# Two-layer diffusion backbone on one core: values in four tiles, pooling partly on VectorE, softmax division moved to the outputs, early products moved to VectorE

## The chip, the core and the metric

The kernel runs on one core of a Trainium2 chip. A core has TensorE (PE, matrix products), VectorE (DVE), ScalarE (ACT), GpSimd (POOL) and SyncE (SP), which here issues nearly all DMAs, one after the other. The metric is the device time of one execution in microseconds; the time before is the median of three runs, 1372.81 us (1372.37 to 1374.88).

## The reference

Two layers work on 1024 latent tokens (a grid of 16 rows by 64 columns) and 256 context tokens, with 1024 features. Cut to what matters here:

```
h  = rmsnorm(x) * (1 + scale) + shift               # modulation from silu(c) @ w_mod
p  = h @ w_in                                       # one projection, split over four mixers
y  = concat(gla(p), neighbourhood_attention(p), s5(p), pool(p)) * silu(gate columns of p)
x  = x + gate * rmsnorm(y @ w_out)

neighbourhood_attention: 4 heads of 64; each latent query reads an 8 x 16 window and the 256 context
  tokens; s = q k + bias, -inf outside the window; p = softmax(s); o = p v; context queries read
  context tokens alone (layer 0 only)
pool: windows 2, 4, 8, 16 (64 features each): (centred_mean(u, w) - u) @ w_pool, times a scale;
  at the ends of the sequence the mean is over the tokens that are there
```

Layer 1 gives no context output.

## The kernel before, in words

Products in float32 are made of three products of a high and a low part each (`hi*hi`, `hi*lo`, `lo*hi`). Features that pass between stages lie in DRAM (`dP` pooling input, `dQ`, `dK`, `dN` queries, keys and values, `dG` gates, `dY` mixer outputs). A layer runs gated linear attention with the modulation products beside it (phase "mods", which reads the silu of the conditioning, `csil`, held in SBUF throughout), the S5 scan, the pooling and gate projections, then phase "na" (L1234), which this change concerns most, and phase "out". The order on each engine comes from a scheduler that lists instructions by priority, and every engine works its list in order: what stands at the head and waits holds up all behind it, SP's DMAs too.

Phase "na" has 4 heads. A job is one head and one block of 128 queries, in the order 0, 1 (context, layer 0 only), 4, 5, 2, 3, 6, 7, 8, 9: 40 jobs in layer 0, 32 in layer 1. Per job: scores on PE (L1331 into `nS`), add of the bias and row minimum on DVE (L1338; L1341 for context blocks), exponential with row sum on ACT (L1343), reciprocal of the sum (L1345) and multiplication of the 128 x 640 probabilities by it on DVE (L1346). Three jobs later PE transposes the probabilities (L1376 into `nT`, three buffers), ACT casts the high part (L1382) and DVE makes the low part (L1383). Per pair of jobs PE multiplies by the values (L1398), ACT copies one half (L1400), and DVE adds the halves into `nay` (L1412). There are 20 pairs in layer 0 and 16 in layer 1.

`na_head` loads a head's keys (L1293), queries (L1299, two buffers) and values: `naV`, one tile 128x10x128 of all ten token blocks, 640 KB, with one buffer (L1302). So the next head's values can be loaded only when the last product of this head has read the tile.

Beside the jobs, one pooling piece (256 tokens, half of the features) is made every four jobs: SP loads the input (L1453, `pu`) and the 128x256 reciprocals of the window lengths (L1455, `piv`, one buffer); POOL makes window sums (L1457 to L1463), multiplies the two halves by `piv` (L1465, L1466) and subtracts the input (L1467). PE, ACT and SP finish the piece (L1476 to L1479). There are 10 pieces in layer 0 and 8 in layer 1. In layer 0, part of the gate projections (L317, L346) fills PE between the jobs.

Two jobs before the end, `out_early` (L393) starts on the first three output tiles: `out_load` (L366) loads parts of `dY` and `dG` (L376) into freed `naK` and `naQ` buffers, multiplies them on POOL (L377), and ACT and DVE make the high and low parts (L379, L380). There are six such products a layer.

Of the kernel before, what the change touches and what calls it, by code (L numbers as in the profile page):

```python
# [12 lines left out]
F32 = mybir.dt.float32  # L13
F32R = mybir.dt.float32r
# [8 lines left out]
SEQ = 1024  # L23
# [16 lines left out]
NH = '11'  # L40
NRM = 0
PS0 = 0
# [27 lines left out]
class Kernel:  # L70
# [72 lines left out]
    def load_consts(self):  # L143
# [16 lines left out]
        self.dG = [self.dram.tile([D, NTOK], F32, name=f"dG{l}") for l in range(DEPTH)]  # L160
        self.dY = [self.dram.tile([D, NTOK], F32, name=f"dY{l}") for l in range(DEPTH)]
        self.dX = self.dram.tile([NTOK, D], F32, name="dX")
        self.dU = [self.dram.tile([NTOK, 256], F32, name=f"dU{l}") for l in range(DEPTH)]
# [9 lines left out]
    def silu_c(self):  # L173

        nc, v = self.nc, self.nc.vector
        cc, th = (self.t([128, 8, 2], "cc", 2) for _ in range(2))
        nc.sync.dma_start(cc, self.a["cc"])
        nc.scalar.activation(th, cc, AF.Tanh, scale=0.5)
        v.scalar_tensor_tensor(th, th, 1.0, cc, op0=ALU.add, op1=ALU.mult)
        v.tensor_scalar(th, th, 0.5, None, op0=ALU.mult)  # L180

        self.csil = self.const.tile([128, 4, 34], F32, name="csil")
        v.memset(self.csil, 0.0)
        for i in range(2):
            v.tensor_copy(self.csil[:, :, 32 * i:32 * i + 2], th.rearrange("p (a b) n -> p a b n", b=2)[:, :, i])

    def modulation(self, l, pieces, raws, width, psum, pool, lag=1):
# [178 lines left out]
    def out_load(self, l, t, dest, k0, n, early=None):  # L366
# [8 lines left out]
        for x, d in ((y, self.dY), (g, self.dG)):  # L375
            self.q(5).dma_start(x, d[l][k0 * 128:(k0 + n) * 128, t * 128:(t + 1) * 128].rearrange("(k p) n -> p k n", p=128))  # L376
        self.eng(4).tensor_tensor(y, y, g, ALU.mult)  # L377
        hi, lo = (x[:, ks] for x in dest)
# [906 lines left out]
    def na_head(self, l, h, last):  # L1285
# [8 lines left out]
        for piece in range(2):  # L1294
# [5 lines left out]
            Q.append(qt)  # L1300
        V = self.t([128, 10, 128], "naV", 1, dtype=F32R)
        nc.sync.dma_start(V.bitcast(F32), self.dN[l][:, h * 128:(h + 1) * 128].rearrange("(t p) e -> p t e", p=128))  # L1302
        if h % 2 == 0:
# [82 lines left out]
    def na_values(self, l, job0, job1, last):  # L1386
# [5 lines left out]
        one = [(b, 0, 128 * a, 128) for a, b in rest]  # L1392
        hi = [(V[:, b, :], o, 0, s, q, n) for b, s, q, n in both + one]
        lo = [(V[:, b, 0:64], o[0:64], 1, s, q, n) for b, s, q, n in both + one]
        todo = hi[:1] + lo[:1] + hi[len(both):] + lo[1:] + hi[1:len(both)]
        for i, (w, out, part, s, q, n) in enumerate(todo):
            x = PT[:, part, s].rearrange("p a q -> p (a q)")[:, q:q + n]
            nc.tensor.matmul(out[:, q:q + n], lhsT=w, rhs=x, start=(i == 0), stop=(i == len(todo) - 1))  # L1398
# [7 lines left out]
        if NRM:  # L1406
            for i, r in enumerate((r0, job1[2])):
                nc.tensor.transpose(ps[0:64, i * 128:(i + 1) * 128], r.to_broadcast([128, 64]), self.ident)
            nc.vector.tensor_tensor(t[0:64], o[0:64], t[64:128], ALU.add)
            nc.vector.tensor_tensor(yc, view(t[0:64]), view(ps[0:64, 0:256]), ALU.mult if NRM == 1 else ALU.divide)  # L1410
        else:
            nc.vector.tensor_tensor(yc, view(o[0:64]), view(t[64:128]), ALU.add)  # L1412
# [15 lines left out]
    def pooling(self, l, last):  # L1428
# [4 lines left out]
        wb, sc = wb[:, 0:256].rearrange("p (m n) -> p m n", m=2), wb[:, 256:258]  # L1433
        nc.sync.dma_start(sc, a["pool_sc"][l])
        nc.sync.dma_start(wb, a["pool_wb"][l].rearrange("m k n -> k m n"))
        PAD = 8
# [3 lines left out]
        for (t0, t1, lo, hi) in pieces:  # L1440
            n = t1 - t0
            W = n + 2 * PAD
            for m in range(2):
# [9 lines left out]
                nc.sync.dma_start(u[:, d0:d1], self.dP[l][m * 128:(m + 1) * 128, c0:c1])  # L1453
                iv = self.t([128, PW], "piv", 1)
                nc.sync.dma_start(iv[:, :n], a["pool_inv"][:, m, t0:t1])  # L1455

# [7 lines left out]
                rr, uu = s4[:, PAD:PAD + n], u[:, PAD:PAD + n]  # L1464
                gp.tensor_tensor(s4[0:64, PAD:PAD + n], s2[0:64, PAD:PAD + n], iv[0:64, :n], ALU.mult)  # L1465
                gp.tensor_tensor(s4[64:128, PAD:PAD + n], s4[64:128, PAD:PAD + n], iv[64:128, :n], ALU.mult)  # L1466
                gp.tensor_tensor(rr, rr, uu, ALU.subtract)  # L1467
                todo.append((m, t0, n, u, rr, wb, sc))
# [63 lines left out]
    def run(self):  # L1532
# [9 lines left out]
        for l in range(DEPTH):  # L1542
# [5 lines left out]
            with self.phase("mods", True) as pool:  # L1548
                psum = self.ps2
                pm = lambda: psum.tile([128, 512], F32, tag="pm", bufs=1, name=self.nm("pm"))  # L1550
                todo = ((1, (2,)),) if last else ((0, (2,)), (1, (1, 0)))
# [45 lines left out]
def _consts():  # L1597
# [40 lines left out]
    out["id32"] = np.tile(np.eye(32, dtype=f), (4, 1))  # L1638
    inv = np.zeros((128, 2, NTOK), f)
    for wi, w in enumerate((2, 4, 8, 16)):  # L1640
        for off, n in ((0, CTX), (CTX, SEQ)):
            t = np.arange(n)
            cnt = np.clip(t - w // 2 + w, 0, n) - np.clip(t - w // 2, 0, n)
            inv[64 * (wi % 2):64 * (wi % 2) + 64, wi // 2, off:off + n] = (f(1.0) / cnt.astype(f))[None]
    out["pool_inv"] = inv
# [96 lines left out]
```

## Time and profile before

| | us | share |
|---|---|---|
| median of three runs | 1372.81 | |
| profiled execution, its own time | 1372.72 | |
| its span | 1370.9 | |
| PE busy | 1252.5 | 91% |
| DVE busy | 913.4 | 67% |
| ACT busy | 582.7 | 43% |
| POOL busy | 202.8 | 15% |

The span is the time between the first and the last instruction of the profiled execution. Shares are means over stages with different limits. DMAs moved 228.99 MB. Phase "na" lies at about 490 to 613 us in layer 0 and 1155 to 1272 us in layer 1; its heads begin (first score minimum) at 494.4, 520.4, 546.7 and 578.9 us, and at 1163.1, 1184.5, 1205.7 and 1232.0 us.

### The profile page before, as it was taken

Reading aid. Unit: us, or ns where it says so; the run is one execution under the profiler, and the core shown is the slowest. Engines: PE = TensorE matmul, PEld = TensorE weight load, DVE = VectorE, ACT = ScalarE, POOL = GpSimd, SP = SyncE. Lnnn points to the kernel's source line nnn. Section 1 sums busy time; section 2 is a strip of 40 time slices with the busy share of each in tenths; the row PEclk is TensorE's granted clock in tenths of the full one; section 3 lists DMA queues with packets and bytes.
Section 4 is the critical chain, followed back from the end, with each engine's and each line's share of the span. In section 5 each row is a group of like instructions: output and inputs, shape, how many; then the busy total and the mean of one; then the engine's idle time right before and its main releaser. Section 6 shows DMA issues by size and latency. Waiting matters only on the chain. (4 is left out here: it accounts for less than half of the span.)

```text
span 1370.9 us, 20412 instructions
## 1 busy us (share of the span) xinstructions
PE 1252.5 (91%) x7102; PEld 1009.2 (74%) x7102; DVE 913.4 (67%) x2269; ACT 582.7 (43%) x1234; POOL 202.8 (15%) x218
## 2 busy tenths in 40 slices
PE   5799999999999999888989999999999989787897
PEld 2698967676777677777778989868767766666676
DVE  2778577546388658774875689596554884877383
ACT  2653433223333347653455642453323333665321
POOL 0100000001100024442410000000212100335220
PEclk9799999999999999999999999999999999989999
DMA  9446686752533277637742475975315434864662
GB/s 330 170 124 223 195 252 177 227 161 77 166 125 117 79 195 187 179 121 234 236 117 91 134 221 187 256 200 165 88 50 184 154 127 145 213 146 131 197 209 89
DMA packets 233846, 228.99 MB, mean 167 GB/s; under 512 B 47144, under 2 KB 196136, under 8 KB 233408
## 3 DMA queue, kind: packets, MB, share of 16 engines
q1 hardware_dynamic: 232144, 225.05, 54.4%
q10 hardware_dynamic: 1584, 2.49, 0.5%
q8 instruction: 59, 0.97, 0.3%
q14 instruction: 59, 0.48, 0.1%
HBM read 157.88 MB, written 69.62 MB: 166 GB/s over the span
## 5 line engine op out<-in xcount | busy, mean ns | idle before, releaser
L317 PE MATMUL pa<-ahi,wh 128*128 128x512 f32 (+1 forms) x664 | 172.3, 386 | 3.3 <-DVE stg L346 1.5
L317 PE MATMUL pa<-ahi,wl 128*128 128x512 f32 (+1 forms) x664 | 165.9, 378 | 0.1
L317 PE MATMUL pa<-alo,wh 128*128 128x512 f32 (+1 forms) x664 | 163.8, 377 | 0.3 <-PEq L1571 0.3
L317 PEld LDWEIGHTS pa<-ahi,wh 128*128 128x128 f32 x664 | 115.4, 192 | 28.5 <-issue 6.0
L317 PEld LDWEIGHTS pa<-alo,wh 128*128 128x128 f32 x664 | 115.8, 192 | 22.5 <-issue 4.7
L317 PEld LDWEIGHTS pa<-ahi,wl 128*128 128x128 f32 x664 | 114.3, 190 | 22.7 <-issue 5.6
L302 POOL TENSOR_TENSOR wl<-w,wh 128x1024 fp32r<-128x1024 f32 (+1 forms) x19 | 46.4, 2445 | 277.7 <-PE pa L317 177.2
L333 PE MATMUL pa<-wh,ahi 128*128 128x256 f32 (+1 forms) x480 | 79.5, 300 | 4.9 <-DVE ahi L260 3.9
L387 PE MATMUL po<-wx,ahi 128*128 128x512 f32 x312 | 79.1, 393 | 2.8 <-DVE stg L473 1.6
L301 ACT CAST wh<-w 128x1024 fp32r<-128x1024 f32 (+1 forms) x51 | 53.8, 1056 | 62.5 <-PE pa L317 39.6
L333 PE MATMUL pa<-wl,ahi 128*128 128x256 f32 (+1 forms) x480 | 79.4, 299 | 0.1
L333 PE MATMUL pa<-wh,alo 128*128 128x256 f32 (+1 forms) x480 | 77.2, 296 | 0.0
L333 PEld LDWEIGHTS pa<-wh,ahi 128*128 128x128 f32 x480 | 66.8, 194 | 10.1 <-issue 3.0
L387 PEld LDWEIGHTS po<-wx,ahi 128*128 128x128 f32 x312 | 58.8, 190 | 16.3 <-ACT ahi L379 2.0
L333 PEld LDWEIGHTS pa<-wl,ahi 128*128 128x128 f32 x480 | 67.5, 194 | 3.6 <-issue 2.5
L333 PEld LDWEIGHTS pa<-wh,alo 128*128 128x128 f32 x480 | 66.2, 193 | 3.3 <-issue 3.0
L1331 PE MATMUL nS<-naK,naQ 128*128 128x256 f32 (+1 forms) x272 | 57.6, 333 | 11.4 <-DVE nast L1338 6.6
L1398 PE MATMUL nT<-naPT,naV 128*128 128x256 f32 (+3 forms) x368 | 58.1, 298 | 9.9 <-DMA naV<-dN 9.2
L1338 DVE CUSTOM_DVE_ANT_0 naP<-nS,nab 128x640 f32<-128x640 f32 (+1 forms) x64 | 50.2, 785 | 18.7 <-PE nS L1331 13.8
L1398 PEld LDWEIGHTS nT<-naPT,naV 128*128 128x128 f32 (+1 forms) x368 | 49.6, 176 | 15.4 <-issue 7.7
L1376 PE MATMUL nT<-c_ident,naP 128*128 128x128 f32 x320 | 51.5, 286 | 9.4 <-DVE nay L1412 3.9
L1383 DVE TENSOR_TENSOR naPT<-nT,naPT 128x512 fp32r<-128x512 f32 (+1 forms) x104 | 56.2, 559 | 5.7 <-ACT naPT L1382 5.3
(396 smaller groups left out, 2550.5 us busy)
## 6 DMA issues: line engine op xcount, KB each, us to landing
w<-in_w_in_dram SPq DMA_DIRECT2D x41, 512.0 KB
wm<-in_w_mod_dram SPq DMA_DIRECT2D x32, 512.0 KB
s5R<-dR SPq DMA_DIRECT2D x16, 960.0 KB
xt<-in_tok_dram SPq DMA_DIRECT2D x20, 512.0 KB
wm<-in_w_mod_dram SPq DMA_DIRECT2D x8, 1024.0 KB
dR<-sp_R SPq DMA_DIRECT2D x16, 512.0 KB
dG<-stg SPq DMA_DIRECT2D x32, 256.0 KB
w<-in_w_out_dram SPq DMA_DIRECT2D x16, 512.0 KB
```

Of the source, the lines that this page charges most:

```text
L301: nc.scalar.copy(hi, raw)
L302: (next(engines) if engines else self.eng(2)).tensor_tensor(lo, raw, hi.bitcast(F32), ALU.subtract)
L317: nc.tensor.matmul(ps[:, :t1 - t0], lhsT=w(k), rhs=x[:, k, t0:t1], start=(i == 0), stop=(i == 23))
L333: nc.tensor.matmul(ps[:, :n], lhsT=x[:, k, t * 128:(t + 1) * 128], rhs=w(k), start=(i == 0), stop=(i == 23))
L387: self.nc.tensor.matmul(o, lhsT=x[:, k], rhs=m(k), start=first and i == 0, stop=last and i == len(todo) - 1)
L1331: nc.tensor.matmul(self.na_s[:, c * 128:(c + n) * 128], lhsT=Qb[:, i, :], rhs=K[:, b * 128:(b + n) * 128], start=(i == 0), stop=(i == 1))
L1338: v.tensor_tensor_reduce(P[:, 0:nk], ps, self.na_b[:, b0:b0 + nk], 1.0, -NEG, ALU.add, ALU.min, nm)
L1376: nc.tensor.transpose(ps[:, i * 128:(i + 1) * 128], P[:, c * 128:(c + 1) * 128], self.ident)
L1383: (nc.gpsimd if RLO == "p" and len(src) < 4 else nc.vector).tensor_tensor(lo, pv, hi.bitcast(F32), ALU.subtract)
L1398: nc.tensor.matmul(out[:, q:q + n], lhsT=w, rhs=x, start=(i == 0), stop=(i == len(todo) - 1))
```

## The change

Five edits. (1) `naV` becomes four tiles: blocks 0 and 1 (`naVc`, two buffers), 2 to 4 (`naVa`), 5 and 6 (`naVb`), 7 to 9 (`naVd`), each with its own load. (2) `NRM = 1`: probabilities are not multiplied by the reciprocal; instead PE transposes the two reciprocals of a pair into the first half of an `nT` tile, ahead of the pair's value products, and DVE multiplies the sum of the two output halves (`nat`) by them. (3) Pooling: one 128x34 load of `piv` a layer instead of one load a piece; on POOL only 64x8 multiplications at the ends of the sequence stay of the last three operations, and two DVE operations of 64x256 a piece scale and subtract. (4) The products of the early output tiles go to DVE. (5) `csil` is stored to DRAM (`dC`) once and loaded again in each phase "mods". Tiles that are held no longer or are smaller free room in SBUF.

```diff
-NRM = 0
+NRM = 1
@@ silu_c
-        self.csil = self.const.tile([128, 4, 34], F32, name="csil")
+        self.csil = self.t([128, 4, 34], "csil", 1)
...
+        nc.sync.dma_start(self.dC, self.csil)
@@ out_load
-        self.eng(4).tensor_tensor(y, y, g, ALU.mult)
+        (nc.vector if early else self.eng(4)).tensor_tensor(y, y, g, ALU.mult)
@@ na_head
-        V = self.t([128, 10, 128], "naV", 1, dtype=F32R)
-        nc.sync.dma_start(V.bitcast(F32), self.dN[l][:, h * 128:(h + 1) * 128].rearrange("(t p) e -> p t e", p=128))
+        parts = ((0, 2, "naVc", 2), (2, 3, "naVa", 1), (5, 2, "naVb", 1), (7, 3, "naVd", 1))
+        V = {}
+        for b, n, tag, bufs in parts:
+            x = self.t([128, n, 128], tag, bufs, dtype=F32R)
+            nc.sync.dma_start(x.bitcast(F32), self.dN[l][b * 128:(b + n) * 128, h * 128:(h + 1) * 128].rearrange("(t p) e -> p t e", p=128))
+            V.update((b + i, x[:, i]) for i in range(n))
@@ na_values
+        if NRM:
+            for i, r in enumerate((r0, job1[2])):
+                nc.tensor.transpose(ps[0:64, i * 128:(i + 1) * 128], r.to_broadcast([128, 64]), self.ident)
...
         if NRM:
-            for i, r in enumerate((r0, job1[2])):
-                nc.tensor.transpose(ps[0:64, i * 128:(i + 1) * 128], r.to_broadcast([128, 64]), self.ident)
             nc.vector.tensor_tensor(t[0:64], o[0:64], t[64:128], ALU.add)
             nc.vector.tensor_tensor(yc, view(t[0:64]), view(ps[0:64, 0:256]), ALU.mult if NRM == 1 else ALU.divide)
@@ pooling
+        iv = self.t([128, 2, 17], "piv", 1)
+        nc.sync.dma_start(iv, a["pool_inv"])
...
-                iv = self.t([128, PW], "piv", 1)
-                nc.sync.dma_start(iv[:, :n], a["pool_inv"][:, m, t0:t1])
...
-                gp.tensor_tensor(s4[0:64, PAD:PAD + n], s2[0:64, PAD:PAD + n], iv[0:64, :n], ALU.mult)
-                gp.tensor_tensor(s4[64:128, PAD:PAD + n], s4[64:128, PAD:PAD + n], iv[64:128, :n], ALU.mult)
-                gp.tensor_tensor(rr, rr, uu, ALU.subtract)
+                for p, x in ((slice(0, 64), s2), (slice(64, 128), s4)):
+                    for c, w, there in ((PAD, 0, t0 == lo), (PAD + n - 8, 8, t1 == hi)):
+                        if there:
+                            gp.tensor_tensor(x[p, c:c + 8], x[p, c:c + 8], iv[p, m, w:w + 8], ALU.mult)
+                    nc.vector.scalar_tensor_tensor(rr[p], x[p, PAD:PAD + n], iv[p, m, 16:17], uu[p], op0=ALU.mult, op1=ALU.subtract)
@@ run, phase "mods"
+                self.csil = self.t([128, 4, 34], "csil", 1)
+                nc.sync.dma_start(self.csil, self.dC)
```

How the order changes is shown at three places; a number behind a tile's name is its instance. The first is SP in layer 1 around the last head's load of the values. Before, the load of `naV` stands behind a load of `piv`:

```order
L376 DMA naK_18567<-dG_88 128x4x128
L1453 DMA pu_18337<-dP_107 128x272
L1231 DMA nab_17612<-in_na_bias_dram 128x256
L1479 DMA dY_90<-pu_18199 128x256
L376 DMA naQ_18573<-dY_90 128x2x128
L1455 DMA piv_18468<-in_pool_inv_dram 128x256
L1302 DMA naV_18221<-dN_97 128x10x128
L1453 DMA pu_18463<-dP_107 128x264
```

After, in the same place, with the four loads spread among the others:

```order
L1308 DMA naVc_18269<-dN_98 128x2x128
L1423 DMA dY_90<-nay_17676 64x1024
L1301 DMA naQ_18266<-dQ_100 64x2x640 x2
L1308 DMA naVa_18271<-dN_98 128x3x128
L1233 DMA nab_17650<-in_na_bias_dram 128x256
L1490 DMA dY_90<-pu_18125 128x256
L378 DMA naK_18624<-dY_90 128x4x128
L378 DMA naK_18624<-dG_88 128x4x128
L1463 DMA pu_18393<-dP_108 128x272
L1308 DMA naVb_18273<-dN_98 128x2x128
...
L1490 DMA dY_90<-pu_18250 128x256
L1308 DMA naVd_18275<-dN_98 128x3x128
```

No load of `piv` stands between them, and the context part stands ahead of the head's second query load.

The second place is DVE at the end of layer 1's jobs. Before, from a multiplication of probabilities (`naP`) on; `stn` and `alo` are low parts of the early output tiles:

```order
L1346 TENSOR_SCALAR naP_18505<-naP_18505,nast_18506 128x640
L1338 ISA naP_18559,nast_18560<-nS_17618,nab_17612 128x640
L1338 ISA nast_18560 128x1
L1345 RECIPROCAL nast_18524<-nast_18524 128x1
L1412 TENSOR_TENSOR nay_17958<-nT_18496,nat_18541 64x2x16x8
L1346 TENSOR_SCALAR naP_18523<-naP_18523,nast_18524 128x640
L1383 TENSOR_TENSOR naPT_18511<-nT_18551,naPT_18511 128x128
L380 TENSOR_TENSOR stn_18566<-naQ_18573,stn_18565 128x256
L1345 RECIPROCAL nast_18560<-nast_18560 128x1
```

After, from the score minimum (L1345 there) of the last job but one on:

```order
L1345 ISA naP_18617,nast_18618<-nS_17656,nab_17650 128x640
L1345 ISA nast_18618 128x1
L379 TENSOR_TENSOR naQ_18630<-naQ_18630 128x256
L1390 TENSOR_TENSOR naPT_18660<-nT_18661,naPT_18660 128x4x128
L379 TENSOR_TENSOR naK_18636<-naK_18636 128x512
L1355 RECIPROCAL nast_18618<-nast_18618 128x1
L382 TENSOR_TENSOR stn_18623<-naQ_18630,stn_18622 128x256
L382 TENSOR_TENSOR alo<-naK_18636,ahi 128x4x128
L1345 ISA naP_18672,nast_18673<-nS_17656,nab_17650 128x512
L1345 ISA nast_18673 128x1
L379 TENSOR_TENSOR naQ_18642<-naQ_18642 128x256
L1417 TENSOR_TENSOR nat_18706<-nT_18609,nat_18706 64x256
```

The multiplications L1346 are gone, and three products with the gates (L379), each of which needs a DMA, stand among the last two score minima and the transposes' low parts.

The third place is PE in layer 1, where a pair's values begin. Before, the rest of the pair's transposes, other work, and the values:

```order
L1376 MATMUL nT_17980<-c_ident,naP_17850 128x128
L1376 MATMUL nT_17980<-c_ident,naP_17868 128x128
L1376 MATMUL nT_17996<-c_ident,naP_17904 128x128 x4
L1331 MATMUL nS_17618<-naK_17700,naQ_17706 128x384 x2
L1331 MATMUL nS_17618<-naK_17700,naQ_17706 128x256 x4
L1331 MATMUL nS_17618<-naK_17700,naQ_17706 128x384 x2
L1398 MATMUL nT_17980<-naPT_17912,naV_17709 128x256
L1398 MATMUL nT_17980<-naPT_17912,naV_17709 64x256
```

After:

```order
L1383 MATMUL nT_18158<-c_ident,naP_18042 128x128
L1383 MATMUL nT_18158<-c_ident,naP_18059 128x128
L1338 MATMUL nS_17656<-naK_17991,naQ_17994 128x384 x2
L1338 MATMUL nS_17656<-naK_17991,naQ_17994 128x256 x2
L1383 MATMUL nT_18173<-c_ident,naP_18097 128x128 x4
L1383 MATMUL nT_18207<-c_ident,naP_18114 128x128 x4
L1405 MATMUL nT_18158<-c_ident,nast_18043 64x128
L1405 MATMUL nT_18158<-c_ident,nast_18060 64x128
L1408 MATMUL nT_18158<-naPT_18102,naVb_17754 128x256
L1408 MATMUL nT_18158<-naPT_18102,naVb_17754 64x256
```

Two transposes of a reciprocal (L1405) come in ahead of the values, into the tile that the rest's transposes used.

## Rows read from the trace of the kernel before

**Rows 1.** Stretches of seven heads: start:end, length, busy PE PEld DVE ACT POOL, clock, DMA.

```profile
494.40:520.40 26.00, 24.28 (x155) 20.05 (x153) 22.36 (x54) 17.57 (x41) 11.24 (x13) 1.00 0.82 204
520.40:546.70 26.30, 24.84 (x161) 20.53 (x161) 22.62 (x58) 17.82 (x46) 9.39 (x14) 1.00 0.68 176
546.70:578.90 32.20, 27.46 (x182) 23.00 (x181) 23.75 (x63) 20.25 (x48) 14.74 (x18) 1.00 0.71 184
578.90:605.50 26.60, 25.40 (x167) 21.30 (x166) 23.29 (x60) 19.91 (x48) 10.62 (x16) 1.00 0.44 132
1184.50:1205.70 21.20, 17.25 (x118) 14.22 (x118) 18.47 (x48) 14.54 (x36) 3.58 (x5) 1.00 0.75 200
1205.70:1232.00 26.30, 21.25 (x118) 18.33 (x118) 19.80 (x48) 16.11 (x39) 8.65 (x12) 0.81 0.62 149
1232.00:1258.30 26.30, 19.66 (x118) 17.31 (x118) 19.41 (x47) 15.53 (x38) 12.69 (x17) 0.87 0.53 145
```

**Rows 2.** PE's waits, 490 to 620 us: waiting line, releaser, total us, times, longest.

```profile
PE nT L1476 <- POOL ps L1467: 3.8, 1, 3.8
PE nT L1398 <- DMA naV<-dN: 3.1, 2, 2.4
```

**Rows 3.** PE's waits, 1155 to 1276 us.

```profile
PE nT L1398 <- DMA naV<-dN: 6.1, 3, 4.4
PE nS L1331 <- DVE nast L1338: 5.6, 10, 1.3
PE nT L1476 <- POOL ps L1467: 2.8, 1, 2.8
PE nS L1331 <- DMA naQ<-dQ: 2.7, 4, 0.9
```

**Rows 4.** The DMA queue's (SP's) waits, 1155 to 1275 us.

```profile
SPq L1455 <- POOL ps L1466: 20.2, 5, 5.7
```

**Rows 5.** Chain that ended last, 1200 to 1272 us: start, us, what.

```profile
1216.45 4.68 DMA naV<-dN
...
1232.47 3.74 DMA naK<-dG
...
1242.07 0.73 POOL ps L1466
1243.21 5.24 DMA naV<-dN
```

**Rows 6.** Lines by form, 490 to 620 us: count, busy, mean ns, idle before.

```profile
L1346 DVE TENSOR_SCALAR naP<-naP,nast 128x640 f32<-128x640 f32 x24 | 18.7, 777 | 0.2
L1412 DVE TENSOR_TENSOR nay<-nT,nat 64x256 f32<-64x256 f32 x20 | 8.3, 417 | 13.1 <-ACT nat L1400 12.7
L1346 DVE TENSOR_SCALAR naP<-naP,nast 128x512 f32<-128x512 f32 x8 | 4.6, 579 | 0.1
L1346 DVE TENSOR_SCALAR naP<-naP,nast 128x256 f32<-128x256 f32 x8 | 2.8, 354 | 0.5
L346 DVE SCALAR_TENSOR_TENSOR stg<-stg,pa 128x256 f32<-128x256 f32 x3 | 1.3, 421 | 0.9 <-ACT stg L345 0.9
```

**Rows 7.** Lines by form, 1155 to 1280 us.

```profile
L1346 DVE TENSOR_SCALAR naP<-naP,nast 128x640 f32<-128x640 f32 x24 | 14.9, 622 | 0.4
L1346 DVE TENSOR_SCALAR naP<-naP,nast 128x512 f32<-128x512 f32 x8 | 5.4, 676 | 0.1
L380 DVE TENSOR_TENSOR alo<-naK,ahi 128x512 fp32r<-128x512 f32 x2 | 1.4, 681 | 0.0
L380 DVE TENSOR_TENSOR stn<-naK,stn 128x512 fp32r<-128x512 f32 x1 | 1.1, 1130 | 0.0
```

**Rows 8.** Timeline of PE around 1200 to 1206 us, two rows of transposes.

```profile
1202.90 0.82 PE L1376 MATMUL nT<-c_ident,naP 128*128 128x128 f32 x6
1204.08 0.66 PE L1376 MATMUL nT<-c_ident,naP 128*128 128x128 f32 x4 [0.35 <-DVE nay L1412]
```

**Rows 9.** Timeline of POOL around 1238 us, one row.

```profile
1238.41 0.87 POOL L1461 TENSOR_TENSOR ps<-ps 128x269 f32<-128x269 f32 x1
```

More of the change, by code (lines that the diff above doesn't have):

```diff
@@ L161, in load_consts @@
         self.dY = [self.dram.tile([D, NTOK], F32, name=f"dY{l}") for l in range(DEPTH)]
+        self.dC = self.dram.tile([128, 4, 34], F32, name="dC")
         self.dX = self.dram.tile([NTOK, D], F32, name="dX")
@@ L1392, in na_values @@
         one = [(b, 0, 128 * a, 128) for a, b in rest]
-        hi = [(V[:, b, :], o, 0, s, q, n) for b, s, q, n in both + one]
-        lo = [(V[:, b, 0:64], o[0:64], 1, s, q, n) for b, s, q, n in both + one]
+        hi = [(V[b], o, 0, s, q, n) for b, s, q, n in both + one]
+        lo = [(V[b][:, 0:64], o[0:64], 1, s, q, n) for b, s, q, n in both + one]
         todo = hi[:1] + lo[:1] + hi[len(both):] + lo[1:] + hi[1:len(both)]
+        if NRM:
+            for i, r in enumerate((r0, job1[2])):
+                nc.tensor.transpose(ps[0:64, i * 128:(i + 1) * 128], r.to_broadcast([128, 64]), self.ident)
         for i, (w, out, part, s, q, n) in enumerate(todo):
@@ L1638, in _consts @@
     out["id32"] = np.tile(np.eye(32, dtype=f), (4, 1))
-    inv = np.zeros((128, 2, NTOK), f)
+    inv = np.zeros((128, 2, 17), f)
+    t = np.r_[0:8, SEQ - 8:SEQ]
     for wi, w in enumerate((2, 4, 8, 16)):
[L1641 to L1644, printed above, removed]
+        cnt = np.clip(t - w // 2 + w, 0, SEQ) - np.clip(t - w // 2, 0, SEQ)
+        at = inv[64 * (wi % 2):64 * (wi % 2) + 64, wi // 2]
+        at[:, 0:16], at[:, 16] = w * (f(1.0) / cnt.astype(f)), 1.0 / w
     out["pool_inv"] = inv
```

## The prediction

> **What bounds the kernel now.** I read the windows by head first, then the waits of PE and of SP, the chain that ended last, and the lines kept apart by shape. In the windows (busy microseconds of PE, weight loads, DVE, ACT and POOL, then the mean granted clock, the DMA share and GB/s) the reader is to see two layers with different limits [rows 1]. In layer 0 PE is busy 24.28 to 27.46 us of heads that last 26.0 to 32.2, since gate projections fill it: 102 of 111 us. Nothing else there is as full. In layer 1, where no filler is left, PE is busy 17.25 to 21.25 us of 21.2 to 26.3, and DVE 18.47 to 19.80: a head of 21.2 us is paced by the round of scores, minimum, exponential and multiplication, and PE waits 5.6 us for the score minimum [rows 3].
>
> Three of the seven heads are longer than their neighbours. The third of layer 0 lasts 32.2 us beside 26.0, 26.3 and 26.6 (mean 26.3): 5.9 over. The last two of layer 1 last 26.3 beside 21.2: 5.1 each. Together 16.1 us [rows 1]. What ends PE's idle time in them is the load of the values: 3.1 us in layer 0 [rows 2] and 6.1 in layer 1, with a longest of 4.4 [rows 3], and the chain runs through that load twice, 4.68 and 5.24 us [rows 5]. Behind the second stands a story of three queues: POOL waits for the gates of an early output tile (3.74 us in the chain), so its pooling multiplication by `piv` ends late at 1242.8, SP stands at the next load of `piv` until then, and `naV` is right behind it, issued at 1243.21 [rows 5]. In that layer SP stands 20.2 us at such loads in five waits [rows 4]. The mean granted clock is 1.00 in five heads, 0.81 and 0.87 in the last two [rows 1]: a part of these two ran at 1.2 instead of 2.4 GHz, after PE had stood. That is inside the 16.1.
>
> **The change part by part.** The sum is made against the profiled execution, 1372.7 us (span 1370.9 and 1.8 around it), which is within 0.1 us of the median, 1372.8.
>
> *Values in four tiles, and no `piv` load a piece.* Each part of `naV` is free when its own blocks have been read, so the next head's first pair finds its blocks 0, 1 and 3 to 6 loaded while the present head still works on 7 to 9, and SP has nothing of POOL's ahead of them. The cost to be removed lies between PE's direct waits, 3.1 + 6.1 = 9.2 us [rows 2, 3], and the whole excess, 16.1. What is late next is the query tile: PE waits 2.7 us for `naQ` in layer 1 [rows 3], whose buffers don't change. So I take -11, the direct waits and a quarter of the rest. Three more DMAs a head on SP, 24 in all, stand in place of 18 loads of `piv`: nothing.
>
> *Division on the outputs and pooling on DVE.* Layer 0 loses 18.7 + 4.6 + 2.8 = 26.1 us of multiplications and gains a second output operation a pair, 20 x 0.417 = 8.3 [rows 6]. For the scale-and-subtract of 64x256 there is no row; the 128x256 one of L346 takes 0.421 [rows 6], and I use it for 20 of them: 8.4. Three products with the gates at the price of the low parts, which read two SBUF tensors too, some 0.42 to 0.68 [rows 6, 7]: 3.3 for six, half of them within these jobs, 1.7. Net -7.7. Layer 1 loses 14.9 + 5.4 = 20.3 [rows 7] and gains 16 x 0.417 + 16 x 0.421 + 3.3 = 16.7: -3.6. In layer 1 DVE is in the pacing round, so I count -3.5 (bounds -3.6 and 0). In layer 0 PE is the limit, so DVE's gain is worth 0 (bound -7.7) as long as PE has filler.
>
> *PE's two added transposes a pair.* A row of six transposes takes 0.82 us and one of four 0.66 [rows 8]: between (0.82 - 0.66)/2 = 0.08 and 0.82/6 = 0.14 each, taken 0.11. Layer 0: 40 x 0.11 = 4.4; layer 1: 32 x 0.11 = 3.5. In layer 1 they lie in PE's 4 to 7 idle us a head: 0. In layer 0 they would add to a full engine; against them, transposes of the probabilities no longer wait for L1346, and PE's 9 us of idle time there are to be filled. I set them against DVE's gain of that layer: 0, bounds -3 and +4.4.
>
> *A longer hold of `nT`.* The transposed reciprocals lie in the tile of the rest of the pair until the second output operation has read them, one operation (0.417) later. With 36 pairs that is 15.0 us if each were waited for, 0 if the other two buffers cover it. Taken +1, nearer to the cover.
>
> *Tails.* The last pooling piece ends each layer's jobs: PE waits 3.8 and 2.8 us for L1467 [rows 2, 3]. Three POOL operations of 0.73 [rows 5] with small gaps, 2.4, go; two edge multiplications of 64x8 (no row; between 0 and 0.73, taken 0.2) and two on DVE, 0.84, come: -1.2 a layer, -2.4 (bounds -6.6, all that PE waits there, and 0).
>
> *Early products on DVE.* Work of 3.3 us a layer is counted above. New is the wait: a load of gates not yet landed now stops DVE, and behind it in DVE's list are the last score minimum and low parts, for which ACT, PE and so the end wait. One stand of the full length costs 3.74, what the chain shows for such a load [rows 5]; there are 12 products. Bounds 0 and 44.9; since SP is freed of its 20.2 us of standing, the loads go out earlier, and I take +1.5 a layer, +3.
>
> *`csil` through DRAM.* No row shows it. The modulation products wait for weights anyway; 0, at most two loads of 3.74 by the row of the gates' load.
>
> Sum: -11 - 3.5 + 0 + 0 + 1 - 2.4 + 3 = -12.9, so 1372.7 - 12.9 = 1359.8 us.
>
> The low part of a `naK` tile took 1130 ns instead of 681 [rows 7] while POOL's L1461 took 0.87 us [rows 9]: both engines slow down when DVE reads two tensors from SBUF beside POOL's work. The Trainium skill says so of the two engines' shared SBUF interfaces (GPSIMD Engine Reference, 8. Key points: contention with VectorE instructions that have two SBUF inputs). The trace agrees, with these numbers. It speaks against the change, which adds only operations of that kind; rival C prices it.
>
> **The rivals.** A: *the queries take the place of the values.* `naQ` has two buffers for two pieces a head, and PE already waits for it [rows 3]. If half of the 11 us comes back there, the sum is -7.4: 1365.3. Against it: in the long heads PE's idle time names `naV` far more than `naQ`.
>
> B, the slower side: *DVE stands at the products.* With no wait at all there the sum would be -15.9; each full stand takes 3.74 away, so from five full stands of the 12 the kernel is slower. With six, one per product of one layer, it is 1372.7 - 15.9 + 22.4 = 1379.2. For it: the products of layer 1 stand in DVE's list ahead of the last score minimum, and the trace has POOL waiting for just these loads. Against: POOL came to them early because it was idle; DVE comes to them when it has worked off its list.
>
> C: *contention.* If the 36 scale-and-subtract operations and 12 products were all stretched by 1130/681 = 1.66 [rows 7], layer 1 alone would pay 16 x 0.28 + 3.3 x 0.66 = 6.7 on the pacing engine, the sum is -6.2, and the time 1366.5. Against: POOL keeps fewer operations, two to four of five to seven a piece besides those at the ends, so there is less to collide with.
>
> D: *the parts come no earlier.* If SP's list holds the four loads until the last block of the old head is read, nothing is gained but small terms: 1371, no change. Against: the order shows the first part ahead of the queries and the last one well behind it.
>
> **How the numbers follow.** Forecast 0.50, A 0.16, C 0.10, D 0.09, B 0.15. A measurement of this kernel tells a change of 0.2% (2.7 us) from none. Forecast, A and C lie beyond that: faster 0.76; D: same 0.09; B: slower 0.15. The lowest sum is the whole excess, DVE's gain in both layers and the tails: -16.1 - 3.6 - 7.7 - 2.4 = -29.8, 1343; the likeliest case's own range is 1350 to 1367 (the excess in full, or the direct waits with the transposes on top). For 8 in 10 I go from 1346 to 1374, which takes in A, C, D and B up to four stands.
>
> **What would show it.** Right: the three long heads shrink to 27 us or less in layer 0 and 22 in layer 1 at clock 1.00; no wait of PE for `naVa` to `naVd` over 1 us; SP no longer stands at `piv`; DVE's busy time falls by some 11 us; PE's waits for the last pooling piece fall below 3 us. Wrong: DVE idle before L379 for a DMA by more than 10 us in the two phases together (B); PE's wait for `naQ` above 8 us (A); mean time of the 64x256 operations above 0.6 us (C). If layer 0 gets longer by about 4 us with the long head gone, the transposes were not covered.

## The result, and the profile after

The changed kernel takes 1382.1 us (median of five runs; four lie between 1378.16 and 1383.63, one of 2001.92 us stands far off and is not in the ratio). The ratio to the kernel before is 1.0061, with an interval of 1.0039 to 1.0083: about 8 us slower, where 13 us faster was forecast and 1374 was the upper end of the range. The profiled execution took 1378.2 us, 5.4 more than that of before.

What was to go did go. PE's waits for `naV` [rows 2, 3] are not in the lists any more, and SP's standing at `piv` [rows 4] is gone; in layer 1 SP stands 9.9 us at the four loads of the values (L1308) instead, until PE has read the old blocks. But PE waits elsewhere. PE's waits of the changed kernel, 490 to 625 us (waiting line, releaser, total us, times, longest), with L1338 the scores, L1345 the score minimum, L1383 the transposes, L1405 those of the reciprocals, L1487 the pooling product and L1418 the second output operation:

```profile
PE nS L1338 <- DVE nast L1345: 4.8, 5, 1.6
PE nT L1487 <- DVE nay L1418: 3.7, 2, 2.1
PE nT L1383 <- DVE nay L1418: 3.6, 2, 1.9
PE nT L1405 <- DVE naPT L1390: 2.7, 2, 2.0
```

And 1160 to 1280 us, the first two:

```profile
PE nS L1338 <- DVE nast L1345: 13.3, 10, 3.8
PE nT L1383 <- DVE naPT L1390: 4.3, 3, 3.0
```

All of these name DVE. In layer 1 the wait for the score minimum was 5.6 us before [rows 3] and is 13.3 now, with a longest of 3.8 for 1.3; e4 will show that the longest wait tells more here than the sum. The eight heads in the changed kernel (start:end, length, busy time of PE, weight loads, DVE, ACT and POOL, then the clock, DMA share, GB/s):

```profile
492.40:519.80 27.40, 25.45 (x161) 22.10 (x160) 18.71 (x51) 16.29 (x39) 7.88 (x15) 0.94 0.69 176
519.80:549.80 30.00, 26.48 (x174) 21.90 (x173) 21.43 (x57) 20.11 (x48) 4.89 (x12) 1.00 0.68 181
549.80:581.40 31.60, 28.24 (x186) 24.31 (x185) 24.91 (x63) 18.55 (x47) 7.53 (x9) 0.95 0.56 153
581.40:610.50 29.10, 25.74 (x169) 21.23 (x167) 20.75 (x55) 18.86 (x45) 4.39 (x9) 1.00 0.37 104
1169.90:1192.60 22.70, 16.45 (x92) 13.62 (x93) 15.06 (x41) 12.51 (x29) 4.68 (x10) 0.78 0.67 179
1192.60:1214.10 21.50, 17.61 (x128) 15.39 (x129) 17.80 (x47) 15.97 (x39) 1.25 (x2) 1.00 0.69 185
1214.10:1240.00 25.90, 19.47 (x127) 17.51 (x127) 18.89 (x50) 15.38 (x36) 3.87 (x6) 0.87 0.56 140
1240.00:1262.90 22.90, 18.89 (x127) 16.98 (x126) 19.39 (x49) 15.26 (x36) 4.50 (x10) 0.93 0.49 138
```

Against [rows 1]: the third head of layer 0 is hardly shorter (31.6 for 32.2), the other three are longer (27.4, 30.0, 29.1 for 26.0, 26.3, 26.6), although DVE is busy less in them. In layer 1 only the last head gains much (22.9 for 26.3). POOL is busy for 1.25 to 7.88 us a head, so it does not lack time. The mean granted clock is below 1.00 in five of the eight heads; before it was in two of the seven shown.

The stall is seen in a stretch of the third head, at the piece that holds DVE longest of the 18. Timeline of the changed kernel, 553 to 559 us (start, us, engine, line, operation, and in brackets idle time and its releaser); the scores that the minimum at 558.52 reads were issued at 553.36:

```profile
553.36 0.87 PE L1338 MATMUL nS<-naK,naQ 128*128 128x384 f32 x4
554.04 0.64 POOL L1465 TENSOR_TENSOR ps<-pu 128x271 f32<-128x271 f32 x1 [10.82 <-DMA pu<-dP]
554.64 2.37 POOL L304 TENSOR_TENSOR wl<-w,wh 128x1024 fp32r<-128x1024 f32 x1
555.02 2.27 DVE L1478 SCALAR_TENSOR_TENSOR ps<-ps,piv,pu 64x256 f32<-64x256 f32 x1
557.09 0.68 POOL L1467 TENSOR_TENSOR ps<-ps 64x256 f32<-64x256 f32 x1
557.80 0.48 DVE L1478 SCALAR_TENSOR_TENSOR ps<-ps,piv,pu 64x256 f32<-64x256 f32 x1 [0.51 <-POOL ps L1467]
558.52 0.81 DVE L1345 CUSTOM_DVE_ANT_0 naP<-nS,nab 128x640 f32<-128x640 f32 x1
559.38 0.83 ACT L1350 ACTIVATE naP<-naP,nast 128x640 f32<-128x640 f32 x1 [2.64 <-DVE nast L1345]
```

DVE comes to a piece's two scale-and-subtracts (L1478) while POOL is at the weights' low part (L304), 2.37 us long, which stands ahead of the pooling sum L1467. The first one, which takes 0.48 us alone, takes 2.27 and ends 0.28 us after L304; the second waits for L1467. The score minimum behind them starts some 4 us after its scores have ended. POOL itself was late because the piece's input was: it stood 10.82 us for the load of `pu`, which SP issued at 551.02.

PE can pay for a stand twice: it waits, and then it runs slower. In layer 1 two scale-and-subtracts start at 1223.43, after 1.09 us of idle time for POOL's L1470. The score minimum follows at 1225.02, and PE, which stood 3.82 us for it (the longest of its waits above), goes on at 1225.91. From then on its granted clock is 0.50 (1.2 instead of 2.4 GHz) for 4 us (columns as above):

```profile
1222.00:1226.00 4.00, 0.18 (x2) 0.09 (x1) 2.82 (x6) 0.88 (x3) 1.99 (x3) 0.79 0.66 200
1226.00:1230.00 4.00, 4.00 (x18) 3.93 (x19) 3.17 (x8) 2.62 (x6) 1.25 (x2) 0.50 0.56 146
```

For all 36 scale-and-subtracts (lines by form, 488 to 625 us and, in the second fence, 1165 to 1280 us: count, busy, mean ns, idle before):

```profile
L1478 DVE SCALAR_TENSOR_TENSOR ps<-ps,piv,pu 64x256 f32<-64x256 f32 x20 | 12.7, 637 | 9.8 <-POOL ps L1477 7.7 <-POOL ps L1470 1.2 <-POOL ps L1467 0.5
```

```profile
L1478 DVE SCALAR_TENSOR_TENSOR ps<-ps,piv,pu 64x256 f32<-64x256 f32 x16 | 9.3, 581 | 4.8 <-POOL ps L1470 2.5 <-POOL ps L1477 1.6 <-POOL ps L1465 0.4
```

They hold DVE for 12.7 + 9.8 + 9.3 + 4.8 = 36.6 us, where the prediction had 15.1 (36 x 0.421) and no wait.

### The profile page after: what moved, and what is told of

Read it like the earlier page. It is cut to its first block, busy times and chain, and to the rows that moved or that the text cites. A ratio compares the mean times of both kernels' runs of the same rounds, so it can differ in the third digit from the quotient of the medians.

```text
span 1376.4 us, 20582 instructions
## 1 busy us (share of the span) xinstructions
PE 1253.6 (91%) x7174; PEld 1016.0 (74%) x7174; DVE 919.0 (67%) x2281; ACT 583.5 (42%) x1234; POOL 151.6 (11%) x176
## 5 line engine op out<-in xcount | busy, mean ns | idle before, releaser
L319 PE MATMUL pa<-alo,wh 128*128 128x512 f32 (+1 forms) x664 | 160.9, 375 | 0.3 <-PEq L1584 0.3
L319 PEld LDWEIGHTS pa<-alo,wh 128*128 128x128 f32 x664 | 116.0, 191 | 22.9 <-issue 4.5
L1338 PE MATMUL nS<-naK,naQ 128*128 128x256 f32 (+1 forms) x272 | 60.3, 344 | 21.5 <-DVE nast L1345 18.1
L304 POOL TENSOR_TENSOR wl<-w,wh 128x1024 fp32r<-128x1024 f32 (+1 forms) x19 | 46.6, 2457 | 271.9 <-PE pa L319 154.0
L335 PE MATMUL pa<-wl,ahi 128*128 128x256 f32 (+1 forms) x480 | 76.4, 294 | 0.1
L1338 PEld LDWEIGHTS nS<-naK,naQ 128*128 128x128 f32 x272 | 43.1, 204 | 34.4 <-DVE nast L1345 27.6
L1383 PE MATMUL nT<-c_ident,naP 128*128 128x128 f32 x320 | 52.8, 289 | 11.5 <-DVE nay L1418 5.0
L1350 ACT ACTIVATE naP<-naP,nast 128x640 f32<-128x640 f32 (+1 forms) x64 | 51.5, 805 | 26.5 <-DVE nast L1345 23.9
L1389 ACT CAST naPT<-nT 128x512 fp32r<-128x512 f32 (+1 forms) x104 | 48.0, 488 | 28.6 <-PE nT L1383 25.3
```

Of the source, the lines that this page charges most:

```text
L304: (next(engines) if engines else self.eng(2)).tensor_tensor(lo, raw, hi.bitcast(F32), ALU.subtract)
L319: nc.tensor.matmul(ps[:, :t1 - t0], lhsT=w(k), rhs=x[:, k, t0:t1], start=(i == 0), stop=(i == 23))
L335: nc.tensor.matmul(ps[:, :n], lhsT=x[:, k, t * 128:(t + 1) * 128], rhs=w(k), start=(i == 0), stop=(i == 23))
L1338: nc.tensor.matmul(self.na_s[:, c * 128:(c + n) * 128], lhsT=Qb[:, i, :], rhs=K[:, b * 128:(b + n) * 128], start=(i == 0), stop=(i == 1))
L1350: nc.scalar.activation(P[:, 0:nk], src, AF.Exp, bias=nm, scale=-1.0, accum_out=l1)
L1383: nc.tensor.transpose(ps[:, i * 128:(i + 1) * 128], P[:, c * 128:(c + 1) * 128], self.ident)
```

## The experiments

Twelve kernels ran. A ratio is to runs of the kernel before made beside them, with its 95% interval; 1% is 13.7 us, and a difference of two ratios is uncertain by 4 to 6 us. Theory 1: DVE stands for POOL at the scale-and-subtract. Theory 2: the division on the outputs costs PE and `nT`. Theory 3: the wait for the values only moved.

| run | what it is | ratio | interval |
|---|---|---|---|
| e1 | values in four tiles, small `piv`, `csil` reloaded; pooling on POOL | 0.9924 | 0.9901 to 0.9946 |
| e2 | division on the outputs, `csil` reloaded | 1.0076 | 1.0051 to 1.0101 |
| e3 | new pooling alone | 1.0000 | 0.9984 to 1.0017 |
| e4 | all, pooling arithmetic back on POOL | 0.9891 | 0.9870 to 0.9912 |
| e5 | `csil` reloaded alone | 1.0019 | 0.9997 to 1.0040 |
| e6 | e4, early products on POOL | 0.9935 | 0.9911 to 0.9959 |
| e7 | all, scale-and-subtract written a step later | 0.9961 | 0.9942 to 0.9980 |
| e8 | e4, `csil` rebuilt | 0.9866 | 0.9833 to 0.9898 |
| e9 | e8 without the division | 0.9881 | 0.9850 to 0.9911 |
| e10 | small `piv` alone, pooling on POOL | 0.9946 | 0.9926 to 0.9966 |
| e11 | division alone, `csil` rebuilt | 1.0065 | 1.0038 to 1.0092 |
| e12 | all but the division | 1.0007 | 0.9981 to 1.0033 |

**e1.** The values in four tiles, with the small `piv` and the reloaded `csil` of the change; the division is left out, the products stay on POOL, and the pooling arithmetic is POOL's as before:

```diff
-                    nc.vector.scalar_tensor_tensor(rr[p], x[p, PAD:PAD + n], iv[p, m, 16:17], uu[p], op0=ALU.mult, op1=ALU.subtract)
+                    gp.tensor_tensor(s4[p, PAD:PAD + n], x[p, PAD:PAD + n], iv[p, m, 16:17].to_broadcast([64, n]), ALU.mult)
+                gp.tensor_tensor(rr, rr, uu, ALU.subtract)
```

> The kernel before with the values in four tiles, csil through DRAM, and one small piv load a layer, but with all pooling arithmetic left on POOL (L1465 to L1467 stay, the factor read as one column). Theory 1 (DVE stands for POOL at the scale-and-subtract, and that ate the values' gain): this has the values' gain and no new DVE work, so 1362 to 1366 us. Theory 2 (the division on the outputs costs PE and nT buffers): also 1362 to 1366. Theory 3 (the values' wait only becomes another wait, the queries' or the scores'): 1370 to 1374, as before.

Measured 0.9924, -10.4 us. Theory 3 falls: the gain that was forecast for the values and `piv`, 11 us, is there.

**e2.** The kernel before with `NRM = 1` and the transposes ahead of the values, as in the change.

> The kernel before with the division moved to the outputs alone (and csil through DRAM, for room). Theory 1: DVE loses more than it gains and nothing waits for POOL, 1368 to 1373 us. Theory 2: the 72 added transposes, which stand ahead of the values and wait for the low part, and the longer hold of nT cost 4 to 9 us, 1377 to 1382. Theory 3: 1371 to 1375.

Measured 1.0076, +10.4 us. The division by itself costs, as theory 2 has it, or else the reload of `csil` does, which was in this kernel too; e11 parts them.

**e3.** The kernel before with the change's pooling.

> The kernel before with the new pooling alone (one piv load a layer, 36 scale-and-subtracts of 64x256 on DVE). Theory 1: DVE stands 10 us or more ahead of these for POOL, score minima come later, 1375 to 1381 us. Theories 2 and 3: the SP queue's standing at piv is gone and POOL does less, 1366 to 1372.

Measured 1.0000, neither range, although DVE does stand 11.6 us in front of the 36 operations, as theory 1 expects. e10 shows why.

**e4.** The changed kernel with the diff of e1.

> The changed kernel with the scale-and-subtract put back on POOL (three operations a piece as before, the factor read as one column of the small piv), all other edits kept. Theory 1: the DVE waits for POOL go, 1363 to 1370 us, faster than both kernels. Theory 2: no more than 2 us from the changed kernel, 1378 to 1382. Theory 3: 1374 to 1378, the difference to before being the early products and the transposes.

Measured 0.9891, -15.0 us, and 23 us faster than the changed kernel (1.0061 - 0.9891 = 0.0170). Two operations a piece on DVE, made three on POOL again, turn the result round. PE's waits of e4, 488 to 625 us, all of them:

```profile
PE nS L1338 <- ACT naP L1350: 1.5, 3, 1.0
PE nT L1488 <- POOL ps L1479: 1.2, 1, 1.2
PE nT L1383 <- DVE nay L1418: 1.1, 2, 0.9
PE nT L1488 <- DVE naPT L1390: 0.2, 1, 0.2
```

Nothing is left of the 4.8 us for the minimum, and the holds of `nT` until L1418 are 1.1 us for 7.3. The heads of layer 0 in e4:

```profile
497.10:519.30 22.20, 22.10 (x153) 19.06 (x151) 16.44 (x47) 16.18 (x40) 6.30 (x10) 1.00 0.77 197
519.30:545.40 26.10, 25.05 (x170) 21.11 (x169) 19.49 (x54) 19.58 (x48) 14.16 (x29) 1.00 0.84 215
545.40:570.70 25.30, 24.52 (x163) 20.41 (x162) 19.66 (x54) 18.63 (x45) 12.19 (x18) 1.00 0.60 162
570.70:595.90 25.20, 24.76 (x175) 21.69 (x174) 17.99 (x50) 17.47 (x44) 9.64 (x17) 1.00 0.51 148
```

PE is busy for 96.4 of 98.8 us, at a clock of 1.00. The third head, 32.2 us before, is 25.3. (Part of the gate projections runs outside these heads in e4, 660 instructions of PE for 690, so not all of the 19.3 us between the two kernels' heads is waiting.)

In layer 1 the jobs, from the first score minimum to the last output operation, last 110.2 us in the changed kernel and 97.1 in e4:

```profile
1169.90:1280.10 110.20, 86.27 (x532) 74.33 (x533) 81.40 (x204) 65.68 (x153) 17.71 (x34) 0.88 0.54 146
1162.20:1259.30 97.10, 78.41 (x529) 67.28 (x530) 71.93 (x188) 65.98 (x153) 34.66 (x58) 0.95 0.61 165
```

PE is busy 7.9 us longer in the changed kernel for nearly the same number of instructions, at a mean clock of 0.88 for 0.95. That is more than half of the 13.1 us between the two. The sum of the waits for the score minimum is not what went. In e4, 1155 to 1285 us, it is:

```profile
PE nS L1338 <- DVE nast L1345: 11.7, 15, 1.6
```

The longest fell from 3.8 to 1.6, the sum only from 13.3 to 11.7. All seven kernels with the division have 10.6 to 13.3 us of this wait in layer 1, and all seven without it 5.0 to 7.6. So its rise from 5.6 us comes with the division and is no measure of the loss.

**e5.** The kernel before with `csil` through DRAM.

> The kernel before with csil stored to DRAM and loaded again in each phase mods, nothing else. In the runs so far all kernels with this edit need 111 to 113 us from the first to the last part of layer 1's linear attention (first L933 to last L959), those without it 106. If the reload is the cause: 105.9 to 112 us in that stretch and 1376 to 1381 us in all. If it is chance or comes from another edit: 106 us and 1371 to 1376.

Measured 1.0019, with an interval that holds 1: by the time alone, inconclusive. By the trace it is in layer 1's linear attention: its first part and its last one in the kernel before, in e5 and in e8 (timeline; a transpose at the head, one at the end, idle time in brackets):

```profile
921.44 0.27 PE L933 MATMUL pb<-c_ident,KB 128*128 128x128 f32 x1
...
1027.15 0.44 PE L959 MATMUL pb<-c_ident,sq 128*128 128x128 f32 x2 [0.19 <-DVE s5st L699]
```

```profile
917.71 0.27 PE L935 MATMUL pb<-c_ident,KB 128*128 128x128 f32 x1
...
1029.27 0.44 PE L961 MATMUL pb<-c_ident,sq 128*128 128x128 f32 x2 [1.98 <-DVE sq L958]
```

```profile
914.06 0.33 PE L939 MATMUL pb<-c_ident,KB 128*128 128x128 f32 x1 [0.18 <-DVE KB L1010]
...
1020.75 0.44 PE L965 MATMUL pb<-c_ident,sq 128*128 128x128 f32 x2 [0.21 <-DVE s5st L705]
```

105.7 us before, 111.6 with the reload, 106.7 with `csil` rebuilt. PE waits 2.0 us for DVE at the end of it in e5, 0.2 in the other two. The stretch is 111 to 113 us in e1, e2, e4, e6, e7, e12 and the changed kernel too, which all reload, and 106 to 107 in the ones that don't. With the load the scheduler lists the modulation's products, the projections and the linear attention's parts in another order. That the order is the cause is argued from the two lists, not shown.

**e6.** e4 with the products on POOL:

```diff
-        (nc.vector if early else self.eng(4)).tensor_tensor(y, y, g, ALU.mult)
+        self.eng(4).tensor_tensor(y, y, g, ALU.mult)
```

> The kernel of e4 (all edits, pooling arithmetic on POOL) with the early output tiles' products on POOL as before. If DVE stands at the products' loads (the rival of the prediction): faster than e4 by 3 us or more, 1350 to 1356. If the products on DVE keep POOL free for the pooling: slower than e4, 1361 to 1366. If neither: 1358 to 1360.

Measured 0.9935: 6 us slower than e4 (0.9935 - 0.9891), a little beyond the uncertainty. The products on DVE are a gain. POOL in e6, timeline 596 to 626 us:

```profile
602.88 0.72 POOL L1479 TENSOR_TENSOR ps<-ps,pu 128x256 f32<-128x256 f32 x1
622.29 0.74 POOL L379 TENSOR_TENSOR naQ<-naQ 128x256 f32<-128x256 f32 x1 [18.69 <-DMA naQ<-dG]
```

POOL stands 18.69 us for one load there. But the last pooling piece of the layer was done by then (L1479 at 602.88), so this stand held up no pooling. How the products on DVE gain is not shown. In the changed kernel DVE is idle only 3.6 us in front of all twelve products (line L379, the share of the gates' loads):

```profile
  DMA naQ<-dG: 2.0, 2
  DMA naK<-dG: 1.6, 1
```

**e7.** The two scale-and-subtracts of a piece are written at the start of the next pooling step:

```diff
-                    nc.vector.scalar_tensor_tensor(rr[p], x[p, PAD:PAD + n], iv[p, m, 16:17], uu[p], op0=ALU.mult, op1=ALU.subtract)
+                    due.append((rr[p], x[p, PAD:PAD + n], iv[p, m, 16:17], uu[p]))
...
+                for x in due:
+                    nc.vector.scalar_tensor_tensor(*x, op0=ALU.mult, op1=ALU.subtract)
+                due = []
```

> The changed kernel with each piece's two scale-and-subtracts written one pooling step (four jobs) later, so that they come later in DVE's list; the same work. Theory 1 in the form that DVE's standing for POOL (14 us of idle time in front of them in the changed kernel) delays the score minima: less idle there and 1366 to 1374 us. In the form that the work itself and the two engines' sharing of SBUF costs the time: idle time falls but the time stays at 1378 to 1384. Theory 2 (the division): no change, 1378 to 1384.

Measured 0.9961, 13.7 us faster than the changed kernel with the same work on the same engines. So some 14 of the 23 us hang on the place in the lists. Lines by form in e7, 488 to 625 us, the main form and the one of the last piece, then 1155 to 1290 us:

```profile
L1455 DVE SCALAR_TENSOR_TENSOR ps<-ps,piv,pu 64x256 f32<-64x256 f32 x18 | 9.6, 533 | 4.1 <-POOL pu L1463 1.9 <-POOL ps L1473 1.7 <-POOL ps L1481 0.3
L1486 DVE SCALAR_TENSOR_TENSOR ps<-ps,piv,pu 64x256 f32<-64x256 f32 x2 | 1.0, 500 | 3.8 <-POOL ps L1481 3.8
```

```profile
L1455 DVE SCALAR_TENSOR_TENSOR ps<-ps,piv,pu 64x256 f32<-64x256 f32 x14 | 7.5, 532 | 1.3 <-POOL ps L1468 1.1
L1486 DVE SCALAR_TENSOR_TENSOR ps<-ps,piv,pu 64x256 f32<-64x256 f32 x2 | 1.0, 500 | 1.0 <-POOL ps L1481 1.0
```

In all the idle time falls from 14.6 to 10.2 us; 4.8 of the 10.2 stand at the last piece (L1486), which comes after the last score minimum. Between the jobs 5.4 us are left (L1455). The mean falls from 637 and 581 ns to 533 and 532. Other instructions move in the lists too when these do, so the 13.7 us are not all shown to be this idle time's. What the other 9.6 us of the 23 are, the added work, its stretching beside POOL or the standing that is left, no run parts.

**e8.** `csil` built again in each phase "mods" from a 128x8x2 tile:

```diff
-                self.csil = self.t([128, 4, 34], "csil", 1)
-                nc.sync.dma_start(self.csil, self.dC)
+                self.csil_make()   # memset and two copies on DVE, from the compact tile
```

> The kernel of e4 with the silu kept in a compact tile (128x8x2) and csil built again from it by three small DVE operations in each phase mods, no DRAM. If the reload of csil costs 4 to 6 us in layer 1's linear attention: 1353 to 1356 us. If the cost is one of the scheduler's order that any new instruction there brings: 1358 to 1360, with the stretch still at 111 us.

Measured 0.9866, median 1354.2 us, the lowest ratio of all and faster than both kernels. Its interval overlaps that of e4, so the 3 us between them are likely by the trace of the stretch, not proved by the time.

**e9.** e8 with `NRM = 0`.

> The kernel of e8 (values in four tiles, early products on DVE, pooling arithmetic on POOL with a small piv, csil rebuilt) with the probabilities multiplied on DVE (L1346) as before. If the division on the outputs gains by shortening DVE's part of a job (net 5.7 us in layer 0, 8.4 in layer 1 by the rows): 1358 to 1364, slower than e8. If the added transposes and the longer hold of nT cost more than that: 1346 to 1352, faster than e8. If neither: 1353 to 1356.

Measured 0.9881: no difference from e8 that the intervals show. Beside the other edits of e8 the division on the outputs is worth nothing that can be told either way, although it takes 14.5 us of work off DVE in layer 0's jobs and 12.0 in layer 1's (94.23 and 85.75 us busy in e9, 79.71 and 73.73 in e8).

**e10.** The kernel before with the small `piv` and the diff of e1.

> The kernel before with one small piv load a layer and all pooling arithmetic still on POOL. Measures what SP's standing at piv is worth without new DVE work. If e3 came out even because two effects cancelled (SP freed, DVE standing): 1362 to 1369. If SP's standing cost nothing: 1371 to 1375.

Measured 0.9946, -7.4 us. e3 differs from it only in the engine of the scale-and-subtract: that costs 7.4 us (1.0000 - 0.9946), and e3 was even because two effects cancelled. In e10 PE's wait for `naV` in layer 1 has fallen from 6.1 us [rows 3] to 0.2, with the values still in one tile; the first and the last line of its waits, 1155 to 1276 us:

```profile
PE nS L1333 <- DVE nast L1340: 5.8, 9, 1.3
...
PE nT L1403 <- DMA naV<-dN: 0.2, 1, 0.2
```

**e11.** e2 with e8's `csil`.

> The kernel before with the division on the outputs, csil rebuilt on DVE instead of reloaded, nothing else: e2 without the reload. If e2's 1.0076 was the division's: 1378 to 1384. If it was mostly the reload's: 1371 to 1376. By the prediction's own sum it would be 1369 to 1373.

Measured 1.0065, +8.9 us: the division's own. PE's waits of e11, 488 to 625 us, the first line, and 1155 to 1290 us, the first and the fourth:

```profile
PE nT L1409 <- DMA naV<-dN: 8.6, 2, 6.3
```

```profile
PE nS L1339 <- DVE nast L1346: 13.0, 15, 2.1
...
PE nT L1409 <- DMA naV<-dN: 2.2, 2, 1.4
```

In layer 0 the wait for the values is 8.6 us where it was 3.1 [rows 2], since SP stands at `piv` as before (19.4 us there). In layer 1 it is 2.2 where it was 6.1 [rows 3], and the wait for the score minimum has risen instead. Beside the other edits of e8 the division costs nothing (e8 against e9), so theory 2 holds only in some surroundings. Which wait makes the 8.9 us here is open.

**e12.** The changed kernel with `NRM = 0`.

> The changed kernel with the probabilities multiplied on DVE as before (no division on the outputs), all else as changed: scale-and-subtract on DVE, values in four tiles, early products on DVE, csil reloaded. If DVE's standing for POOL is the loss by itself: 1377 to 1385 us, as slow as the changed kernel or slower, since DVE has more to do. If the loss needs the division too (the transposes and the hold of nT together with the standing): 1364 to 1372.

Measured 1.0007, between the two expectations: slower than e9, which has POOL scale, by 1.0007 - 0.9881 = 0.0126 (17 us; some 3 of it the reload), faster than the changed kernel by 7.4. So the scale-and-subtract on DVE costs without the division, and the two together cost more. Why is open. A part of it can be read: with the division, a standing DVE also holds up the second output operation, on which the `nT` buffers wait. Waits that name the last output operation are 7.3 us in layer 0 of the changed kernel, 3.7 in e12 and 1.1 in e4.

## Why the prediction was wrong

The step that failed is the one named "Division on the outputs and pooling on DVE", in its pooling half: 20 and 16 scale-and-subtracts at 0.421 us, 15.1 us of work and no wait. They take 36.6 us of DVE, 22.0 of work and 14.6 of standing. Their price in time is 7.4 us alone (e3 - e10) and 23 us beside the other edits (changed kernel - e4). In the kernel before all of this chain was POOL's, and a slow POOL held up its own chain and SP's loads of `piv`, but not DVE. Split between the engines, each piece makes DVE wait for POOL's sums, in a list whose next entry is often a score minimum. I asked what is queued behind a waiting DVE only for the products with the gates, and not for the operations that read what POOL had just made. The prediction also put no price on PE's clock after such a stand, which e4 shows in layer 1.

That the operations on DVE are the loss is shown by undoing them (e4) and by adding them (e3 against e10, e12 against e9). That standing is how they lose it is in part argued. The sum of the standing does not set the price: it is 14.6 us in the changed kernel, 11.6 in e3, 10.2 in e7 and 8.2 in e12, for a loss of 23, 7, some 10 and some 14 us (the last two reckoned from e4 and, less the reload, from e9). Which score minimum a stand holds up, and what PE still has to do then, must matter too; no run parts that.

The prediction's own signs say the same. The long heads did not shrink to 27 and 22 us, and DVE's busy time, which was to fall by some 11 us, rose from 913.4 to 919.0. Rival B's sign did not come (3.6 us idle in front of the products, 10 asked for), so that its 1379.2 us lies near the measured time by luck. Rival C's came in layer 0 (0.637 us, 0.6 asked for).

Point by point:

- *Values and `piv`*, -11: right in size (e1 -10.4 with the reload in it). But 7.4 of it comes with the small `piv` load alone (e10), so most was SP's standing and not the single buffer. e1 and e10 differ by 3 us, less than their intervals can tell.
- *Division*, 0 in layer 0 and part of -3.5 in layer 1: nothing beside the other edits of e8, +8.9 alone, +7.4 in the changed kernel. DVE's saving was real (e8 beside e9) and bought no time that the runs can tell. What the transposes cost PE by themselves was not measured; the heads of layer 0 in e4, which have them, are shorter than before all the same.
- *Early products*, +3: the wait was right (3.6 us of idle DVE), the sign was not. They gain 6 us (e4 against e6); how is open. Rival B, which put the slower side here, named the right engine and the wrong instructions.
- *Longer hold of `nT`*, +1: 7.3 us of PE's waits in layer 0 of the changed kernel, where DVE stood, and 1.1 in e4, where it did not: about what was forecast, without the standing.
- *`csil`*, 0, for which the prediction had no row: layer 1's linear attention is 6 us longer in every kernel with the reload. In the whole time about 3 us, at the edge of what the runs tell.
- *Contention*, rival C, 1366.5: it was there (2.27 us for a 0.48 us operation), beside POOL's 2.37 us low part of the weights, and 0.93 to 1.05 us beside its pooling sums. On DVE it is the smaller part: 22.0 us of work instead of 17.3 (36 x 0.48), beside 14.6 of standing.
- *Tails*, -2.4, were not measured by themselves. In layer 0 the wait of 3.8 us for L1467 [rows 2] is replaced by 3.7 us for L1418.

Along the chain of kernels the sum is: small `piv` -7.4 (e10), values with the reload -3.0 (e1), division +1.5 (e6), early products -6.0 (e4), scale-and-subtract on DVE +23.3 (changed kernel): +8.4. It depends on the order in which the edits are added, as e3, e11 and e12 show.

## What to carry to other kernels

Before work is moved from an idle engine to a busy one, ask what the busy engine then waits for: an operation that reads another engine's fresh result costs its wait, and the wait of everything behind it in that list, even if the work is small. Here the chain of small operations was better left whole on POOL, which had time. Ask too what PE's granted clock does after the stand. And where several edits are made together, run each undone: here the two operations a piece on DVE took 23 us, and all the rest had given 15.

## What the runs showed of the hardware

A scale-and-subtract of 64x256 on DVE has two inputs in SBUF and takes 0.47 to 0.52 us in 30 of the changed kernel's 36 cases. The other six ran beside an operation of POOL on SBUF, and each ended 0.27 or 0.28 us after that operation, whatever its length: one took 2.27 us beside POOL's 2.37 (L304), four took 1.04 to 1.05 beside 0.72 to 0.73 (L1471), one 0.93 beside 0.61 (L1467). POOL's operations were not longer than usual (2.40 is the median of L304). It looks as if DVE did not share the time with POOL but waited for its end. The stretch seen before was of another kind: 1.13 us for 0.68 [rows 7], while POOL's operation was longer too (0.87 us [rows 9], where 0.63 is the median of that line in layer 1).
